# Values turned to token-major on VectorE in 32x32 blocks instead of on TensorE

## The chip, the cores and the metric

One core of one Trainium2 chip runs the whole kernel. A core has a matrix engine (TensorE, PE in the profile), two elementwise engines (VectorE, DVE; ScalarE, ACT), a third for small jobs (GpSimd, POOL), and queues that start transfers (SyncE, SP). Each engine takes its instructions in the order in which they were written for it. The metric is the device time of one execution in microseconds (us). Before the change the median of three runs is 1335.77 us (1335.68 to 1336.22).

## The reference, cut to what matters

A two-layer block over 272 tokens (16 learned ones and 256 of the input; the reference pads them to 384 and masks the padding) with 1024 features. In each layer a normalised input is multiplied by a wide matrix, and the slices of the product feed three branches:

```python
proj = (hn @ w_in).astype(F32)
rq, rk, rv, rg, hq, hf, hi, hg, dq, dk, dv, mg = jnp.split(proj, offs, axis=-1)
o_ret = retention(rq, rk, rv, rg, ...)       # 4 heads, values of 256
o_hg  = hgrn2(hq, hf, hi, hg, lb, ...)       # 8 heads, gated recurrence
o_da  = diff_attention(dq, dk, dv, ...)      # 8 heads, two softmax maps each
y = sum(sigmoid(mg) * (branches @ w_branch)) @ w_out
```

A convolutional feed-forward part with inner width 2816 follows, and a last norm after the second layer. What matters here are the values `rv`, `hi` and `dv`, 1024 features each per layer. Every branch ends in a sum over tokens, "scores times values" (`einsum('bhqk,bkhe->bqhe', s, vc)` and the like), so the values must lie with tokens on the partitions.

## The kernel before, in words

All activations lie feature-major: 128 features on the partitions, 272 tokens along the row. `products` (L780) computes one pair of feature tiles: for each of 8 input tiles and each of the two outputs (16 weight tiles) it issues three matmuls of 272 columns (L801 to L803), since each weight tile is split into a rounded part `whi` and a rest `wlo`. Weights come in chunks of 8 tiles: a transfer into `wraw`, an ACT copy to `whi`, a DVE subtraction to `wlo` (L524 to L526); `wraw` has three buffers, `whi` and `wlo` four each (L516 to L518). Two chunks serve one call of `products`.

A value pair comes out of `products` into PSUM. `values` (L1271) copies it to `vsrc` (128 partitions, two tiles of 272 tokens) and calls `to_tokens` (L837), which turns the first 256 tokens: four 128x128 blocks. The last 16 tokens go another way: POOL copies them to `tails`, and `tail_tokens` (L846) turns those of all heads together on PE. There are four value pairs each of `rv`, `hi` and `dv` per layer, so 24 calls of `to_tokens` in the kernel. They write `rvt` (read by `ret_head`, L911) and `vt` tiles (read by `hg_outputs`, L1106, and `da_head`, L1159).

The work of the branches runs in between the products. `hg_heads` (L949) handles four heads in seven levels (`LEVELS`, L34): at each level PE makes small block products into `lev` (L992), DVE copies parts of them out into `near` or `at`, and then DVE multiplies parts of `hq` and `hf` in place by running decays `tot` (L1074 to L1084); the next level's block products read what was multiplied.

The order of instructions isn't written out but planned on the host before the kernel is issued. Each operation becomes an `_Op` with an engine, an estimated cost and a key (a due time in us on a clock that counts the products only). `order` (L354) plays the five engines forward: an engine takes the ready operation that can start first, and of several the one with the lowest key. A result needed on another engine counts as there 0.4 us later (`CROSS`, L263). The costs are fixed formulas (L478 to L495): a DVE operation 0.068 us plus 1.042 ns per element of a row, a main product group of three matmuls 3 x (columns/2400 + 0.003) us, and

```python
            elif method == "transpose":
                cost = 0.11
```

whatever the engine. The weight chunks have keys 6 us before they are due (`LEAD`, L519), the operations of `to_tokens` about 1 us after the end of their product (L807, L1275); those of the branches are spread over the stretch from `+name` to `!name` in `ORDER` (L58, `behind` and `settle`, L1242 and L1256), and one branch part of a chain starts only after the one before it has been planned. Whatever the plan believed, on the chip each engine keeps the planned order and waits where a result is late. Where the plan keeps track of overlaps (`_span`, L286), it treats a view as the whole stretch of the row between its first and last element.

PSUM has two buffers for small products (`bank`, L589), used in turn by the transposed values, the levels, scores and means.

Of the kernel before, what the change touches and what calls it, by code (L numbers as in the profile page):

```python
# [14 lines left out]
AF = mybir.ActivationFunctionType  # L15
# [4 lines left out]
P = 128  # L20
# [526 lines left out]
def _trace(ctx, tc, plan, a, depth, probe):  # L547
    nc = tc.nc
    act = _Engine(plan, nc.scalar, "act", 0.094, 0.833e-3)
    dve = _Engine(plan, nc.vector, "dve", 0.068, 1.042e-3)  # L550
    pe = _Engine(plan, nc.tensor, "pe", 0.0, 4 / 2400)
# [15 lines left out]
    def new(pool_, shape, dt, tag, bufs, name):  # L567
        serial[0] += 1
        return plan.tile(pool_, shape, dt, tag, bufs, f"{name}_{serial[0]}")
# [16 lines left out]
    def temp2(tag, bufs=2):  # L586
        return temp(2 * T, tag, bufs).rearrange("p (a t) -> p a t", a=2)

    def bank(name):  # L589
        return new(bp, [P, 512], F32, "bank", 2, name)  # L590
# [34 lines left out]
    ident = const[:, C_IDENT : C_IDENT + P]  # L625
# [210 lines left out]

    def to_tokens(src, vt, e):  # L837

        pt = bank("vt").rearrange("p (f c e) -> p f c e", f=2, c=2)
        for f in range(2):  # L840
            for c in range(2):
                pe.transpose(pt[:, f, c, :], src[:, f, c * P : (c + 1) * P], ident)
        for f in range(2):
            act.activation(vt[:, :, e + f * P : e + (f + 1) * P], pt[:, f], AF.Copy)

    def tail_tokens(tails):  # L846

# [28 lines left out]
    for li in range(depth):  # L876
# [389 lines left out]
        def block(name):  # L1266
            if name not in st:
                st[name] = slot4(name)
            return st[name]

        def values(ps, vt, e):  # L1271

            src = temp2("vsrc")
            evacuate(src, ps)
            plan.key += 2.0  # L1275
            to_tokens(src, vt, e)
            return src
# [57 lines left out]
        for name, j in ORDER:  # L1335
# [18 lines left out]
            elif name[0] == "*":  # L1354
# [4 lines left out]
                else:  # L1359
                    t = st["rg" if n == "b0" else "hg"]  # L1360
# [6 lines left out]
            if name in BASE:  # L1367
# [18 lines left out]
                elif name in ("dq", "dk"):  # L1386
                    t = block(f"{name}{j // 2}")
# [3 lines left out]
                elif name == "rv":  # L1391
# [3 lines left out]
                    src = values(ps, st["rvt"][j // 2], (j % 2) * 2 * P)  # L1395
# [4 lines left out]
                elif name in ("hi", "dv"):  # L1400
# [7 lines left out]
                    src = values(ps, st[f"{n}t{b}"], (j % 2) * 2 * P)  # L1408
# [6 lines left out]
                else:  # L1415
                    t = block(f"{name}{j // 2}")
# [31 lines left out]
            elif name == "fi":  # L1448
# [9 lines left out]
                c = temp2("two_b")  # L1458
# [8 lines left out]
                c = c[:, :, first:]  # L1467
# [43 lines left out]
```

## Time and profile before

| | us |
|---|---|
| median of three runs | 1335.77 |
| the profiled execution | 1335.99 |
| its span, first to last instruction | 1334.2 |
| PE busy | 1324.1 |
| DVE busy | 962.0 |
| ACT busy | 813.7 |
| POOL busy | 82.8 |

The span is the profiled execution without some 1.8 us around it. The engines work beside each other, so the busy times don't add up; the engine whose work and waits fill the span sets the time. In the rows, L496 is the line of the helper through which nearly all DVE, ACT, POOL and small PE instructions are issued, so that they must be told apart by the tiles that they write and read (`out<-in`), not by the line. PE matmuls overlap each other in the record: a row gives how long one was under way, while the chain of work gives by how much each moved the end.

### The profile page before, as it was taken

The numbers are of one execution on the slowest core, as the hardware profiler recorded it, in microseconds if no ns is written. First come the engines' busy times: TensorE is split into PE (matmuls) and PEld (weight loads), VectorE is DVE, ScalarE is ACT, GpSimd is POOL, SyncE is SP. The second block draws the span as 40 slices with busy tenths as digits, with TensorE's granted clock in tenths as the row PEclk, the third lists the DMA queues.
The fourth block names the chain that finished last, engine by engine and source line by source line (L and its number), as shares of the span: only waits on it lengthen the run. The fifth ranks groups of instructions, "written<-read, shape, count | busy, mean of one in ns | idle before, by whom it ended". The sixth has DMA issues, their size and how long they took to land.

```text
span 1334.2 us, 28652 instructions
## 1 busy us (share of the span) xinstructions
PE 1324.1 (99%) x11734; PEld 1296.1 (97%) x11734; DVE 962.0 (72%) x1628; ACT 813.7 (61%) x1371; POOL 82.8 (6%) x162
## 2 busy tenths in 40 slices
PE   9999999999999999999999999999999999999998
PEld 9999999999999999999999999999999999999986
DVE  7575777697676789786564757776985867898753
ACT  6747454756576567665446474547566775776643
POOL 5000000000010020000030000000011100200000
PEclk9999999999999999999999999999999999999999
DMA  7644544443544545555555445434445446466653
GB/s 269 192 143 157 161 160 127 137 148 127 175 142 159 174 157 176 180 169 184 176 177 178 157 148 170 161 127 143 143 150 169 143 157 204 143 205 189 194 189 109
DMA packets 60754, 219.05 MB, mean 164 GB/s; under 512 B 6864, under 2 KB 6992, under 8 KB 60624
## 3 DMA queue, kind: packets, MB, share of 16 engines
q1 hardware_dynamic: 60336, 216.71, 49.9%
q8 instruction: 92, 1.51, 0.5%
q10 hardware_dynamic: 288, 0.52, 0.1%
q14 instruction: 38, 0.31, 0.1%
HBM read 216.16 MB, written 1.05 MB: 163 GB/s over the span
## 4 chain that ended last, share of the span: by engine, by line
PE 94%; DVE 4%; issue 1%; ACT 0%; DMA 0%; SPq 0%; DVEq 0%
PE main L801 27%; PE main L802 27%; PE main L803 27%; PE lev L992 2%; PE fo L1311 2%; PE fo L1313 2%; PE fo L1312 2%; DVE two_b L496 1%; DVE wlo L496 1%; PE ds L1176 1%; PE ms L496 1%; PE do L496 1%; PE ro L496 1%; PE ho L496 1%; PE vt L496 1%
## 5 line engine op out<-in xcount | busy, mean ns | idle before, releaser
L801 PE MATMUL main<-xh,whi 128*128 128x272 f32 (+1 forms) x2368 | 694.0, 293 | 0.0
L802 PE MATMUL main<-xl,whi 128*128 128x272 f32 (+1 forms) x2368 | 677.5, 286 | 2.4 <-DVE xl L496 2.4
L803 PE MATMUL main<-xh,wlo 128*128 128x272 f32 (+1 forms) x2368 | 677.4, 286 | 0.3 <-DVE wlo L496 0.2
L496 DVE TENSOR_TENSOR wlo<-wraw,whi 128x1024 fp32r<-128x1024 f32 (+1 forms) x406 | 496.5, 1228 | 203.7 <-ACT whi L496 202.6
L496 ACT ACTIVATE whi<-wraw 128x1024 fp32r<-128x1024 f32 (+1 forms) x406 | 426.4, 1052 | 235.3 <-PE main L802 164.6
L802 PEld LDWEIGHTS main<-xl,whi 128*128 128x128 f32 x2368 | 446.2, 188 | 3.7 <-DVE xl L496 3.0
L801 PEld LDWEIGHTS main<-xh,whi 128*128 128x128 f32 x2368 | 445.6, 188 | 1.6
L803 PEld LDWEIGHTS main<-xh,wlo 128*128 128x128 f32 x2368 | 445.1, 188 | 1.4 <-DVE wlo L496 1.3
L496 DVE SCALAR_TENSOR_TENSOR two_b<-main,small,two_b 128x256 f32<-128x256 f32 (+2 forms) x144 | 65.4, 487 | 30.0 <-ACT two_b L496 28.3
L496 ACT ACTIVATE two_b<-main,small 128x272 f32<-128x272 f32 (+1 forms) x72 | 37.3, 565 | 28.6 <-PE main L803 28.6
L496 POOL TENSOR_TENSOR y<-h,rstd 128x272 f32<-128x272 f32 x32 | 34.8, 1120 | 317.6 <-ACT rstd L496 317.6
L802 PE MATMUL main<-glo,whi 128*128 128x272 f32 x176 | 50.8, 289 | 0.0
L803 PE MATMUL main<-ghi,wlo 128*128 128x272 f32 x176 | 50.7, 288 | 0.0
L801 PE MATMUL main<-ghi,whi 128*128 128x272 f32 x176 | 50.6, 288 | 0.0
L496 ACT ACTIVATE vsrc<-main 128x544 f32<-128x544 f32 x24 | 15.0, 626 | 40.0 <-PE main L803 39.9
L801 PE MATMUL main<-b0hi,whi 128*128 128x272 f32 (+1 forms) x128 | 38.1, 298 | 0.0
L801 PE MATMUL main<-b1hi,whi 128*128 128x272 f32 (+1 forms) x128 | 38.0, 297 | 0.0
L496 POOL COPY tails<-vsrc 128x32 f32<-128x32 f32 x32 | 8.4, 277 | 464.2 <-ACT vsrc L496 464.2
L802 PE MATMUL main<-ylo,whi 128*128 128x272 f32 (+1 forms) x128 | 36.6, 286 | 0.0
L802 PE MATMUL main<-b2lo,whi 128*128 128x272 f32 (+1 forms) x128 | 36.6, 286 | 0.0
L802 PE MATMUL main<-b1lo,whi 128*128 128x272 f32 (+1 forms) x128 | 36.6, 286 | 0.0
L803 PE MATMUL main<-b0hi,wlo 128*128 128x272 f32 (+1 forms) x128 | 36.6, 286 | 0.0
(248 smaller groups left out, 1968.4 us busy)
## 6 DMA issues: line engine op xcount, KB each, us to landing
wraw<-in_w SPq DMA_DIRECT2D x402, 512.0 KB, 3.4
h<-in_h SPq DMA_DIRECT2D x4, 272.0 KB, 5.3
dec<-in_dec SPq DMA_DIRECT2D x2, 544.0 KB, 5.4
wraw<-in_w SPq DMA_DIRECT2D x4, 256.0 KB, 4.4
const<-in_const SPq DMA_DIRECT2D x1, 937.0 KB, 8.4
gain<-in_gl SPq DMA_DIRECT2D x1, 512.0 KB, 5.1
out<-y ACTq DMA_DIRECT2D x2, 256.0 KB, 2.8
out<-y SPq DMA_DIRECT2D x2, 256.0 KB, 2.8
```

What stands on the lines that cost most here:

```text
L496: self.plan.add(self.name, lambda: f(*args, **kw), cost, outs, ins, args[2] if method == "activation" else None)
L801: nc.tensor.matmul(o, wh, hi, start=first, stop=False)
L802: nc.tensor.matmul(o, wh, lo, start=False, stop=False)
L803: nc.tensor.matmul(o, wl, hi, start=False, stop=last)
L992: nc.tensor.matmul(o, keys, x, start=True, stop=True)
L1176: nc.tensor.matmul(ss[m][:, at : at + nk], q[half, hd, q0 : q0 + P], k[half, hd, :nk], start=True, stop=True)
L1311: nc.tensor.matmul(o, gh, wh, start=False, stop=False)
L1312: nc.tensor.matmul(o, gl, wh, start=False, stop=False)
L1313: nc.tensor.matmul(o, gh, wl, start=False, stop=end)
```

## The change

`to_tokens` no longer uses PE, PSUM and ACT. A 256-token, two-tile block of `src` is taken as 4 x 4 groups of 32 partitions by 32 token columns. For each pair (i, j) one DVE instruction reads the 32 partitions of group i, token columns j of each of the 2 x 2 blocks, turns the four 32x32 blocks, and writes them to the partitions of group j, feature columns i. That makes 16 instructions of 32 partitions by 128 elements for each call, reading `vsrc` and writing `vt` or `rvt` directly.

```diff
     def to_tokens(src, vt, e):
 
-        pt = bank("vt").rearrange("p (f c e) -> p f c e", f=2, c=2)
-        for f in range(2):
-            for c in range(2):
-                pe.transpose(pt[:, f, c, :], src[:, f, c * P : (c + 1) * P], ident)
-        for f in range(2):
-            act.activation(vt[:, :, e + f * P : e + (f + 1) * P], pt[:, f], AF.Copy)
+        lanes = [slice(32 * i, 32 * i + 32) for i in range(4)]
+        to = vt[:, :, e : e + 2 * P].rearrange("p c (f e) -> p f c e", f=2)
+        x = src[:, :, : 2 * P].rearrange("p f (c t) -> p f c t", c=2)
+        for i in lanes:
+            for j in lanes:
+                dve.transpose(to[j, :, :, i], x[i, :, :, j])
```

The planner and its costs are as before, so each of the 16 instructions is planned at 0.11 us, and the whole order is planned anew.

## The prediction

> **What bounds the kernel now.** I read the page first: span, busy times, chain.
>
> ```profile
> span 1334.2 us, 28652 instructions
> PE 1324.1 (99%) x11734; PEld 1296.1 (97%) x11734; DVE 962.0 (72%) x1628; ACT 813.7 (61%) x1371; POOL 82.8 (6%) x162
> ...
> PE 94%; DVE 4%; issue 1%; ACT 0%; DMA 0%; SPq 0%; DVEq 0%
> ```
>
> PE is at work for 99% of the span and holds 94% of the chain that ended last. So whatever is taken off PE's queue comes off the time, one for one, as long as PE then has nothing to wait for. Second, the waits of PE:
>
> ```profile
> PE main L802 <- DVE xl L496: 2.4, 3, 1.3
> PE warm L496 <- POOL ones_d L496: 1.0, 1, 1.0
> PE main L803 <- DVE wlo L496: 0.2, 1, 0.2
> ```
>
> PE hardly ever waits for VectorE today (2.4 + 0.2 us), although VectorE is busy for 72% of the span. That is what the change puts at stake: it takes work off the bound engine and gives more work to the one that feeds it. Third, the chain of waits around a call, with the first and the last call in it:
>
> ```profile
> 76.88 0.44 PE vt L496 x4
> ...
> 161.81 0.12 PE main L803
> 161.94 0.44 PE vt L496 x4
> 162.38 0.13 PE main L801
> ...
> 1013.14 0.44 PE vt L496 x4
> ```
>
> The four transposes of a call move the end by 0.44 us and stand between main matmuls of 0.12 to 0.13 us without a gap.
>
> **What the change removes.** The instructions of the turned values:
>
> ```profile
> L496 PE MATMUL vt<-const,vsrc x96: 270/272/273, 76.7 to 1013.3; 128*128 128x128 f32 x96
> ...
> L496 ACT ACTIVATE vt<-vt x32: 368/380/405, 77.4 to 1013.9; 128x256 f32<-128x256 f32 x32
> ...
> L496 ACT ACTIVATE rvt<-vt x16: 363/381/388, 175.7 to 868.2; 128x256 f32<-128x256 f32 x16
> ```
>
> 96 transposes are 24 calls, so PE gets back 24 x 0.44 = 10.6 us, the whole gain. The 48 ACT copies (48 x 0.38 = 18 us) go from an engine at 61%; I cost them at nothing, since PE's list above has no wait for ACT. The `bank` buffer that each call held is free for levels and scores, also worth nothing, since PE's waits name no PSUM buffer. [...]
>
> **What it adds.** 24 x 16 = 384 DVE instructions of 32 partitions by 128 elements. No transpose runs on DVE today; the nearest rows are copies of just that shape, and the longer ones for the price of a column:
>
> ```profile
> L496 DVE COPY at<-lev 32x128 f32<-32x128 f32 x8 | 2.3, 282 | 2.1 <-PE lev L992 2.0
> ...
> 202.32 0.28 DVE L496 COPY at<-lev 32x128 f32<-32x128 f32 x1 [0.20 <-PE lev L992]
> 202.53 0.67 DVE L496 TENSOR_TENSOR hq<-hq,tot 128x512 f32<-128x512 f32 x1
> ...
> L496 DVE TENSOR_TENSOR wlo<-wraw,whi 128x1024 fp32r<-128x1024 f32 x402 | 492.9, 1232 | 202.6 <-ACT whi L496 201.5
> L496 DVE TENSOR_TENSOR hf<-hf,tot 128x544 f32<-128x544 f32 x12 | 8.7, 727 | 3.8 <-PE lev L992 3.7
> ```
>
> The copy is under way for 0.28 us, but the next instruction, which doesn't need it, starts 0.21 us after it. A column costs (1232 - 727)/(1024 - 544) = 1.05 ns. A turned block can't give its first row before its 32nd column is in, so I add 32 columns, 0.03 us, to the 0.21: **0.24 us each**, an estimate from these rows. Lower end 0.21 (the turning costs nothing), upper end 0.28 + 0.03 = 0.31 (each waits for the end of the one before). At 0.24 a call is 3.9 us, all 24 are 93 us, and DVE comes to 962 + 93 = 1055 us, 80% of the span. On average that fits; what matters is where the calls lie, and that the planner reckons with 0.11 x 16 = 1.8 us a call. What it foresees it can place (it moves branch work back and lets PE go on with products); what it doesn't, 16 x 0.13 = 2.1 us a call, makes DVE late against the order that both engines keep.
>
> Busy time by stage, first layer, cut at the starts of the calls:
>
> ```profile
> core 0: us, PE busy (x) PEld busy (x) DVE busy (x) ACT busy (x) POOL busy (x), PEclk, DMA share, GB/s
> 76.60:108.00 31.40, 31.40 (x586) 30.12 (x585) 23.51 (x40) 15.06 (x31) 0.64 (x4) 1.00 0.39 129
> 161.80:175.10 13.30, 13.30 (x110) 13.30 (x109) 7.63 (x12) 7.93 (x16) 0.81 (x3) 1.00 0.48 164
> 175.10:198.90 23.80, 23.80 (x478) 22.88 (x477) 19.92 (x34) 12.36 (x28) 1.61 (x5) 1.00 0.48 161
> 198.90:215.00 16.10, 16.10 (x176) 15.66 (x175) 12.76 (x23) 8.23 (x16) 0.00 (x0) 1.00 0.36 106
> 255.00:271.00 16.00, 16.00 (x132) 16.00 (x131) 11.03 (x21) 12.98 (x26) 0.81 (x3) 1.00 0.47 156
> 342.80:366.00 23.20, 23.20 (x189) 23.20 (x187) 12.26 (x10) 13.12 (x20) 1.41 (x4) 1.00 0.54 184
> ...
> 842.30:866.00 23.70, 23.70 (x478) 22.79 (x477) 19.90 (x34) 12.27 (x28) 1.67 (x6) 1.00 0.49 162
> ```
>
> The calls per stretch are 2, 2, 3, 1, 2, 2, and VectorE's idle time 7.9, 5.7, 3.9, 3.3, 5.0 and 10.9 us. The last row is the third again in the second layer, the same within 0.1 us, so I work one layer out and double it. How late VectorE may be is read where PE needs it soonest, at the levels of `hg_heads`: the multiplication of `hf` ends, then the next level starts on PE.
>
> ```profile
> 190.74 0.72 DVE L496 TENSOR_TENSOR hf<-hf,tot 128x544 f32<-128x544 f32 x1
> 194.31 0.72 DVE L496 TENSOR_TENSOR hf<-hf,tot 128x544 f32<-128x544 f32 x1
> ...
> 192.75 0.67 PE lev L992 x52
> 196.24 0.67 PE lev L992 x52
> ```
>
> 192.75 - 191.46 = 1.3 us and 196.24 - 195.03 = 1.2 us: a cushion of **1.2 us**. Beyond it, the level stands at the head of PE's queue and all main matmuls wait behind it. The `wlo` chunks have a larger cushion (four buffers of eight tiles, each tile three matmuls of 0.125 us, so 3 us a chunk), and I cost them at nothing; if that cover went, main matmuls would wait at L803.
>
> Per layer, then:
>
> - 161.8 to 198.9, two `hi` and three `rv` calls, the last three among the levels of the second four heads. Idle 5.7 + 3.9 = 9.6 us; foreseen 5 x 1.8 = 8.8 us, so 0.8 us is left. Unforeseen 5 x 2.1 us; but the levels rank first (their keys are overdue, they start only when the previous part is planned), so about one call's worth of transposes slips behind the last level, where it makes no level late. 4 x 2.1 - 0.8 - 1.2 = **6.4 us**. Lower end 0 (most slips behind the levels), upper end 5 x 2.1 - 2.0 = 8.5.
> - 76.6 to 108, two `hi` calls among the levels of the first four heads: 2 x 3.9 = 7.8 in 7.9 us of idle time, so VectorE catches up, but a call can be late at once by 2.1 - 1.2 = 0.9 us. I take that once, **0.9** (0 to 1.8).
> - 198.9 to 215, one call, 3.9 in 3.3: counted as the call that slips, **0**. 255 to 271, two `dv` calls: foreseen 3.5 in 5.0, the unforeseen 4.2 against 1.5 left and 1.2 of cushion, 1.5 at most; no levels lie here, so **0.5**. 342.8 to 366: 7.8 in 10.9, **0**.
>
> 7.8 us a layer, 15.6 us in all, against 10.6 gained: +5.0 us on the profiled execution's 1335.99 (its span and 1.8 us around it), so 1341.0; that execution lies 0.2 us over the median of 1335.77, and I say **1341 us**. The same sum with 0.21 us each (1.6 unforeseen: 4.4 + 0.4 + 0, 9.6 in both layers) gives 1335, with 0.28 (2.7: 8.8 + 1.5 + 1.5, 23.6) 1349.
>
> **The rivals.** *Faster:* the extra VectorE time lies in idle time after all. For it: VectorE idles for 202.6 us ahead of `wlo`, for want of `whi` (row above), and the planner fills such gaps with transposes while the levels go first; against it: in 175.1 to 198.9 only 3.9 us are idle for three calls. PE then gets its 10.6 us and waits no more than now: 1335.99 - 10.6 = 1325. It decides when PE's new waits stay under 5.3 us a layer. *Serial transposes:* each instruction pays its whole latency, 0.31 us, 5.0 us a call, 3.2 unforeseen. 4 x 3.2 - 2.0 = 10.8, with 2.0 and 2.0 in the other two stretches 14.8 a layer, 29.6 - 10.6 = +19: 1355. For it: the 0.28 us of the copy. Against it: the 0.21 us to its successor, and that the 16 write separate places. [...] *No change:* the two sides cancel, as at 0.21 us each, 1335.
>
> **How the numbers follow.** About 0.2% (2.7 us) is what a measurement of this kernel can tell from no change. Forecast, waits of 7 to 12 us a layer (1339 to 1349): 0.38. Faster, all or most hidden (1325 to 1333): 0.34. Cancelling within 0.2%: 0.12. Serial, or late for another reason by more than 12 us a layer (1350 and over): 0.16. So slower 0.54, same 0.12, faster 0.34. The likeliest case's own range is 1338 to 1349; the range over the cases runs from just above the full gain, 1326, to the serial sum, 1355. A freshly planned order may add a few us of either sign that no row here prices.
>
> **What would show it.** PE's instructions fewer by 96 and no `vt<-const,vsrc` among them; 384 DVE transposes, 0.21 to 0.24 us from start to start; DVE busy near 1055. Among the waits of PE `lev` for `hf`, `hq` or `near` should be new, in the stretches that answer to 161.8 to 215 and 829 to 882, some 6 us each, and `main L803` for `wlo` still small. I am wrong if PE's idle time stays near 10 us (then faster), if the transposes stand 0.3 us or more apart (then the serial sum), or if PE's new waits are for `wlo`.

## The result and the profile after

The changed kernel takes 1383.64 us (median of four runs, 1382.57 to 1385.62) where the kernel before takes 1335.72 (with a fourth run beside the three above): 1.0359 times as long, 95% interval 1.0346 to 1.0371. That is 47.9 us slower, where 5 us slower was forecast, and far above the range's upper end of 1355. The profiled execution is 1384.09 us. The first lines of its page, with the shares of the chain that ended last:

```profile
span 1382.3 us, 28773 instructions
PE 1329.8 (96%) x11638; PEld 1296.0 (94%) x11638; DVE 1072.3 (78%) x2012; ACT 802.7 (58%) x1323; POOL 84.0 (6%) x162
...
PE 77%; DVE 18%; issue 2%; ACT 1%; DMA 0%; SPq 0%; DVEq 0%; ACTq 0%
```

PE issues the 96 instructions fewer, and yet it is busy 5.7 us longer than before and idle for 52.5 us (1382.3 - 1329.8) instead of 10.1. VectorE now holds 18% of the chain instead of 4%. Whom PE waits for (total us, times, longest):

```profile
PE main L803 <- DVE wlo L496: 13.9, 13, 1.8
PE lev L992 <- DVE hq L496: 11.3, 4, 3.5
PE lev L992 <- DVE hf L496: 7.2, 6, 1.3
...
PE main L802 <- DVE xl L496: 2.4, 3, 1.3
PE ms L496 <- DVE hsl L496: 2.3, 1, 2.3
...
```

Before, the list held the `xl` row and 0.2 us for `wlo`. The level waits are those that the prediction looked for; the largest single row is the one for `wlo`, which it costed at nothing. The added instructions, by their tile (duration min/median/max in ns), and VectorE in order of time at the first call and ahead of the levels of the second four heads (start, length in us):

```profile
L496 DVE STREAM_TRANSPOSE vt<-vsrc x256: 292/303/309, 76.7 to 1067.1; 32x128 f32<-32x128 f32 x128
```

```profile
76.65 5.04 DVE L496 STREAM_TRANSPOSE vt<-vsrc 32x128 f32<-32x128 f32 x16
81.73 1.22 DVE L496 TENSOR_TENSOR wlo<-wraw,whi 128x1024 fp32r<-128x1024 f32 x1
82.87 0.72 DVE L496 TENSOR_TENSOR hq<-hq,he 128x544 f32<-128x544 f32 x1
...
172.86 5.05 DVE L496 STREAM_TRANSPOSE vt<-vsrc 32x128 f32<-32x128 f32 x16
...
183.55 2.18 DVE L496 STREAM_TRANSPOSE rvt<-vsrc 32x128 f32<-32x128 f32 x7
185.76 0.73 DVE L496 TENSOR_TENSOR hq<-hq,he 128x544 f32<-128x544 f32 x1
```

Sixteen transposes take 5.04 us: (5.04 - 0.30)/15 = 0.316 us from start to start, and 0.30 us long each, so one begins only when the one before has ended. Often a whole call stands as one block, ahead of a `wlo` chunk and of the multiplication of `hq` that a level waits for. What PE does meanwhile, by stretches (us, busy us and instructions of each engine, then the granted TensorE clock):

```profile
core 0: us, PE busy (x) PEld busy (x) DVE busy (x) ACT busy (x) POOL busy (x), PEclk, DMA share, GB/s
80.00:84.10 4.10, 1.91 (x55) 1.72 (x56) 4.00 (x9) 0.48 (x2) 0.00 (x0) 1.00 0.03 8
84.10:87.50 3.40, 3.40 (x56) 3.34 (x43) 3.33 (x7) 1.66 (x4) 0.76 (x4) 0.50 0.78 265
183.00:186.50 3.50, 0.04 (x1) 0.00 (x0) 3.39 (x12) 0.94 (x2) 0.00 (x0) 1.00 0.23 95
186.50:189.90 3.40, 3.36 (x74) 3.30 (x75) 3.22 (x10) 1.71 (x3) 0.32 (x1) 0.50 0.02 5
285.50:288.90 3.40, 3.40 (x18) 3.40 (x17) 3.33 (x5) 0.71 (x2) 0.00 (x0) 0.50 0.27 59
```

From 183.0 to 186.5 PE stands still while VectorE works without a pause, and in the 3.4 us that follow PE runs at half its clock. The same comes after other waits: six stretches, one of them of 6.8 us, 23.8 us in all, at a granted clock of 0.50. So in these places PE first waited and then worked slowly, which no term of the prediction held.

### The profile page after: what moved, and what is told of

It reads as the page before. It is cut to its first block, busy times and chain, and to the rows that moved or that the text cites. A ratio compares the mean times of both kernels' runs of the same rounds, so it can differ in the third digit from the quotient of the medians.

```text
span 1382.3 us, 28773 instructions
## 1 busy us (share of the span) xinstructions
PE 1329.8 (96%) x11638; PEld 1296.0 (94%) x11638; DVE 1072.3 (78%) x2012; ACT 802.7 (58%) x1323; POOL 84.0 (6%) x162
## 4 chain that ended last, share of the span: by engine, by line
PE 77%; DVE 18%; issue 2%; ACT 1%; DMA 0%; SPq 0%; DVEq 0%; ACTq 0%
PE main L801 22%; PE main L803 22%; PE main L802 22%; DVE wlo L496 5%; DVE vt L496 4%; DVE rvt L496 2%; PE fo L1311 1%; PE fo L1313 1%; PE fo L1312 1%; DVE two_b L496 1%; DVE hq L496 1%; PE ds L1176 1%; DVE hf L496 1%; PE do L496 1%; PE ho L496 1%
## 5 line engine op out<-in xcount | busy, mean ns | idle before, releaser
L803 PE MATMUL main<-xh,wlo 128*128 128x272 f32 (+1 forms) x2368 | 681.2, 288 | 13.9 <-DVE wlo L496 13.9
L496 DVE STREAM_TRANSPOSE vt<-vsrc 32x128 f32<-32x128 f32 x256 | 77.5, 303 | 6.9 <-ACT vsrc L496 3.5
L496 POOL COPY tails<-vsrc 128x32 f32<-128x32 f32 x32 | 11.8, 383 | 497.7 <-ACT vsrc L496 491.8
L992 PEld LDWEIGHTS lev<-hq,hf 128*32 128x32 f32 (+1 forms) x1248 | 18.5, 118 | 23.3 <-DVE hq L496 9.7
L496 DVE STREAM_TRANSPOSE rvt<-vsrc 32x128 f32<-32x128 f32 x128 | 38.7, 302 | 1.7
L992 PE MATMUL lev<-hq,hf 128*32 128x16 f32 (+2 forms) x1248 | 20.9, 198 | 19.1 <-DVE hq L496 11.3
```

Source lines behind the costliest of these rows:

```text
L496: self.plan.add(self.name, lambda: f(*args, **kw), cost, outs, ins, args[2] if method == "activation" else None)
L803: nc.tensor.matmul(o, wl, hi, start=False, stop=last)
L992: nc.tensor.matmul(o, keys, x, start=True, stop=True)
```

## The experiments

Two theories came first. **A, the order:** the planner prices a transpose at 0.11 us, so it places VectorE's work wrongly; with the true price it would place it where it hurts no one. **B, the room:** VectorE has no place for 5 us a call in the stretches where the calls lie, whatever the order. Beside them stood the question which of the prediction's terms failed, the price of a transpose or the waits that a given price makes.

**The true price for the planner.** Only the order can change:

```diff
-                cost = 0.11
+                cost = 0.315 if self.name == "dve" else 0.11
```

> The changed kernel, with the planner told 0.315 us for a DVE transpose (their spacing in the changed kernel's trace) in place of 0.11. Theory A, the order is to blame (VectorE is late against an order made for 1.8 us a call where it takes 5.0): with true costs the order has room, PE's waits for hf, hq and wlo go, time 1330 to 1348. Theory B, capacity (VectorE is busy for 19.4 of 20 us at 180 to 200, so no order helps): 1365 to 1385.

1372.85 us, 1.0276 (1.0261 to 1.0292) of the kernel before. Of the 48 us, 11 come back. Two of PE's waits, and VectorE in order of time between two calls of the second stretch:

```profile
PE main L803 <- DVE wlo L496: 16.1, 15, 5.3
...
PE lev L992 <- DVE hq L496: 3.2, 1, 3.2
```

```profile
204.52 5.05 DVE L496 STREAM_TRANSPOSE rvt<-vsrc 32x128 f32<-32x128 f32 x16
209.59 2.42 DVE L496 TENSOR_TENSOR wlo<-wraw,whi 128x1024 fp32r<-128x1024 f32 x2
...
212.02 5.05 DVE L496 STREAM_TRANSPOSE rvt<-vsrc 32x128 f32<-32x128 f32 x16
```

The levels wait less and the weight chunks more: two whole calls now stand between the `wlo` chunks. A planner that knows the price moves the wait, and gets rid of little of it. A is worth 11 us in this order.

**The same order, other VectorE work.** Three kernels keep every line of the plan, with its price of 0.11, and put something else in the place of the 16 transposes. The first makes one transpose of 128 partitions by 512 elements of the first and nothing of the other 15; the second makes 16 copies of the same shape; the third makes the one whole transpose and five of the small ones.

```diff
-        for i in lanes:
-            for j in lanes:
-                dve.transpose(to[j, :, :, i], x[i, :, :, j])
+        turn = [lambda: nc.vector.transpose(to, x)] + [lambda: None] * 15
+        for n, (i, j) in enumerate((i, j) for i in lanes for j in lanes):
+            plan.add("dve", turn[n], 0.11, [to[j, :, :, i]], [x[i, :, :, j]])
```

```diff
-                dve.transpose(to[j, :, :, i], x[i, :, :, j])
+                out, src_ = to[j, :, :, i], x[i, :, :, j]
+                plan.add("dve", lambda out=out, src_=src_: nc.vector.tensor_copy(out, src_), 0.11, [out], [src_])
```

```diff
-        for i in lanes:
-            for j in lanes:
-                dve.transpose(to[j, :, :, i], x[i, :, :, j])
+        turn = lambda out, src_: (lambda: nc.vector.transpose(out, src_))
+        for n, (i, j) in enumerate((i, j) for i in lanes for j in lanes):
+            out, src_ = to[j, :, :, i], x[i, :, :, j]
+            run = turn(to, x) if n == 0 else turn(out, src_) if n % 3 == 0 else lambda: None
+            plan.add("dve", run, 0.11, [out], [src_])
```

> The changed kernel's order kept to the instruction on PE, ACT, POOL and SP; the 16 transposes of a call replaced by one of 128 partitions by 512 elements, issued at the place of the first. It leaves out the exchange between the lane groups, so the values are not fully turned. A and B alike (VectorE's time is the cause): 24 calls of about 0.75 us, PE's new waits gone, 1325 to 1329. Theory C, the newly planned order is poor in itself, whatever the transposes take: above 1345. Its one duration beside that of the 16 gives the price of a column and the fixed price: at 1.05 ns a column 0.18 fixed and 0.72 us in all; if the turning itself is slow, over 1 us.

> The changed kernel's order kept; each transpose replaced by a DVE copy of the same 32x128 piece between the same lane groups, at the same planned cost. It leaves out the turning inside the blocks. If the turning makes the instruction slow: copies 0.21 us from start to start as in the kernel before, 3.4 us a call, and the time falls by about half of the loss, to 1345 to 1360. If the small SBUF-to-SBUF shape makes it slow: 0.31 us and 1380 to 1385.

> The changed kernel's order kept on every engine; of the 16 transposes of a call the first is one of 128 by 512 (0.63 us), five more are issued as they stand and ten are left out, so that the values are not fully turned: 0.63 + 5 x 0.315 = 2.2 us a call, 0.4 us more than the 1.76 that the planner foresees. In this same order 0.63 us a call gave 1325.5, 3.7 gave 1355.0 and 5.04 gave 1383.6. If the loss is what goes beyond the foreseen 1.76 us: 24 x 0.4 = 10 us at most, less the cushion, so 1325 to 1330. If every us on VectorE counts, foreseen or not (a straight line through the three points from 0.63 on): 1340.

The whole transpose: 1325.46 us, 0.9922 (0.9907 to 0.9937). The copies: 1355.04, 1.0140 (1.0123 to 1.0157). One whole and five small: 1330.67, 0.9960 (0.9946 to 0.9975). The page of the whole transpose and its waits:

```profile
span 1323.9 us, 28414 instructions
PE 1313.6 (99%) x11638; PEld 1285.4 (97%) x11638; DVE 975.5 (74%) x1652; ACT 802.5 (61%) x1323; POOL 81.5 (6%) x162
```

```profile
PE main L802 <- DVE xl L496: 2.4, 3, 1.3
...
PE main L803 <- DVE wlo L496: 0.2, 1, 0.2
```

These are PE's waits of the kernel before. So the new plan by itself does no harm, and without VectorE's extra time the kernel gains 10.4 us: the 10.6 of the prediction. PE does here the same 11638 instructions as in the changed kernel, which makes this the kernel to subtract: of the 58.4 us between the two spans, 42.2 are PE's idle time (52.5 against 10.3) and 16.2 are PE taking longer over the same work (1329.8 against 1313.6).

What one call costs VectorE, from its order of time in the whole and in the copied kernel:

```profile
77.11 0.70 DVE L842 STREAM_TRANSPOSE vt<-vsrc 128x512 f32<-128x512 f32 x1
77.74 1.18 DVE L496 TENSOR_TENSOR wlo<-wraw,whi 128x1024 fp32r<-128x1024 f32 x1
```

```profile
77.11 3.70 DVE L845 COPY vt<-vsrc 32x128 f32<-32x128 f32 x16
```

0.63 us to the next start for the whole one, 3.70 for the copies ((3.70 - 0.22)/15 = 0.232 us each), 5.04 for the transposes, and for one whole and five small 0.63 + 5 x 0.316 = 2.2. With one order this gives the time against the dose:

| VectorE per call, us | time, us | above the whole transpose | per us of VectorE time added since the row above (24 calls) |
|---|---|---|---|
| 0.63 | 1325.46 | | |
| 2.2 | 1330.67 | 5.2 | 5.2 / 37.7 = 0.14 |
| 3.70 | 1355.04 | 29.6 | 24.4 / 36.0 = 0.68 |
| 5.04 | 1383.64 | 58.2 | 28.6 / 32.2 = 0.89 |

The 2.2 of the second row is added up; at the first call its trace has 2.34 us to the next start (76.78 to 79.12), and with that the rates are 0.13 and 0.75. Up to about 2 us a call, what the plan reckons with (1.8), the time is nearly free; beyond that most of every microsecond ends up in the span. The stretch that holds 8 of a layer's 12 calls, first in the whole, then in the copied, then in the changed kernel:

```profile
161.00:300.00 139.00, 139.00 (x1423) 135.95 (x1422) 112.18 (x218) 80.57 (x146) 5.15 (x17) 1.00 0.44 146
```

```profile
161.00:300.00 139.00, 131.87 (x1345) 127.24 (x1344) 122.93 (x307) 74.15 (x123) 4.60 (x15) 1.00 0.41 136
```

```profile
161.00:300.00 139.00, 123.34 (x1251) 118.49 (x1251) 122.29 (x278) 66.87 (x109) 4.32 (x14) 0.98 0.39 123
```

VectorE's own work there is 112.2 - 8 x 0.63 = 107.1 us of 139. With 8 x 5.04 us it is 147.5: more than the stretch has. That is B, and it holds at any order that leaves this work in the stretch. But it is no more than 8.5 us a layer of the loss, 17 of 58, and the copies, 107.1 + 29.6 = 136.8, would fit and still cost PE 7.1 us in this window. In both overloaded kernels VectorE is busy for 122 to 123 us only: it waits in turn (in the changed kernel 4.7 us for `whi` from ACT and 5.4 us for PE are its longest waits here), so the room that is left isn't all used.

**Later, and out of the way.** The true price, the transposes due 15 us later, and a second source buffer for the third and fourth pairs, so that a late turn doesn't hold up the product behind it:

```diff
-            src = temp2("vsrc")
+            src = temp2(tag)      # "two_a" for the later pairs of hi and rv
...
+            plan.key += 15.0
             to_tokens(src, vt, e)
+            plan.key -= 15.0
```

> As e1_priced (true cost of a transpose in the planner), and the transposes' keys 15 us later, so that they rank behind wlo and fill idle time; the sources of the third and fourth pair of hi and rv lie in the two buffers of another tile (two_a), so that a waiting transpose holds up no evacuation. Theory P, the place in the order (in e1_priced two calls of 5 us each stood ahead of the wlo that PE waited for): 1335 to 1350. Theory B, no room: from 161 to 300 us of the kernel before VectorE is busy for 105 us, and the eight calls there take 40 more, 145 against 135 us of PE's work: at least 10 us a layer, 1350 to 1370.

1369.84 us, 1.0254 (1.0239 to 1.0269): 14 of 48 us back at best, 3 of them by the later dates and the second buffer together. The stretch of the first two calls is clean now, and the loss lies behind it (columns as above):

```profile
76.00:112.00 36.00, 36.00 (x622) 34.71 (x621) 33.65 (x76) 18.26 (x34) 0.92 (x5) 1.00 0.36 119
163.00:214.00 51.00, 44.91 (x582) 43.44 (x580) 48.32 (x109) 19.68 (x32) 3.38 (x7) 1.00 0.39 126
214.00:255.00 41.00, 36.41 (x346) 34.66 (x347) 35.45 (x85) 17.05 (x31) 0.00 (x0) 0.88 0.37 119
255.00:330.00 75.00, 69.19 (x531) 67.77 (x531) 65.31 (x151) 45.20 (x85) 3.38 (x13) 0.95 0.40 129
```

PE is idle for 0, 6.1, 4.6 and 5.8 us in the four. So the two orders made with the true price bring back 0.23 and 0.29 of the loss; no other order was tried, so what the best order could bring is not shown.

**One kind of value alone.** The calls of one branch are turned on VectorE, those of the other two on PE as before:

```diff
-    def to_tokens(src, vt, e):
+    def to_tokens(src, vt, e, kind):
+        if not (kind[:2] == "dv"):      # or "hi", or "rv"
...
+            return
```

> Only the eight dv calls on VectorE, the hi and rv calls on PE and ACT as before, costs as in the changed kernel. From the places where the changed kernel fell behind: about 6 and 1 us a layer, so 1335.7 + 14 = 1350 (1345 to 1354). By the prediction's term for the dv calls (0.5 us a layer against 1.8 gained): 1333.

> Only the eight hi calls on VectorE, planned at 0.11 us as in the changed kernel. From where the changed kernel fell behind: about 4.5 us a layer among the first levels, and 0.9 gained a layer at the second two calls, where no level lies: 1335.8 + 7 = 1343. By the prediction's terms (0.9 us a layer and part of 6.4, against 3.5 gained): 1334 to 1340.

> Only the eight rv calls on VectorE, planned at 0.11 us. If the parts add up: 48 for all, less 10.7 for dv (measured) and 7 for hi, leaves 30: 1366. If the lateness of the hi calls just ahead is carried into the levels (the parts don't add up): 1350 to 1360. By the prediction's term (at most 6.4 us a layer against 1.8 gained): 1345.

| turned on VectorE | time, us | ratio (interval) | against before | waits per layer, with the 1.8 us that PE gains | the prediction's term |
|---|---|---|---|---|---|
| `dv` | 1346.5 | 1.0079 (1.0064 to 1.0094) | +10.6 | 7.1 | 0.5 |
| `hi` | 1350.7 | 1.0112 (1.0096 to 1.0127) | +14.4 | 9.0 | 0.9 and a part of 6.4 |
| `rv` | 1357.95 | 1.0161 (1.0144 to 1.0178) | +21.7 | 12.6 | the rest of 6.4 |

The three losses add up to 46.7 us, the whole kernel's 47.9: each branch's calls make their own loss, and none needs the others. (`hi` alone missed what was expected of it, 1343, and with it the 1366 for `rv` "if the parts add up": they do add up, with 14.4 for `hi` in place of 7.) What PE waits for most in each, `dv`, `hi`, `rv`:

```profile
PE main L803 <- DVE wlo L496: 3.6, 4, 1.8
PE ms L496 <- DVE hsl L496: 3.5, 3, 2.3
```

```profile
PE lev L1000 <- DVE hq L496: 8.2, 4, 2.2
```

```profile
PE main L803 <- DVE wlo L496: 8.7, 11, 1.7
```

With `dv` there is no level near the calls, but a norm of the branch outputs (`ms`), whose squares VectorE splits into `hsl`: a call in front of that makes PE as late as one in front of a level. With `hi` it is the levels nearly alone, with `rv` the weight chunks most of all.

**The price of a transpose by its form.** One kernel for durations alone. `hi` calls are made of four instructions of 32 partitions by 512 elements, `rv` calls of four of 128 by 128, `dv` calls of one of 128 by 512 and sixteen short ones that stay in their own lanes:

```diff
+        forms = {"h": [(to[i], x[i]) for i in lanes],
+                 "r": [(to[:, :, :, i], x[:, :, :, i]) for i in lanes],
+                 "d": [(vt[i, 0, e + 32 * n : e + 32 * n + P], src[i, 0, 32 * n : 32 * n + P]) for i in lanes for n in range(4)]}[kind[0]]
...
```

> A look at durations alone; the values are left unturned in part, so its time says nothing. hi calls: 4 instructions of 32 partitions by 512; rv calls: 4 of 128 partitions by 128 in the changed kernel's pattern of 32-element pieces; dv calls: one of 128 by 512, then 16 of 32 partitions by 128 in one piece on their own lanes. If few lanes or the crossing of lane groups make the small ones slow, 128 by 128 stands under 0.25 us apart; if the short pieces do, the 128 in one piece; if each transpose pays a fixed 0.18 us when another follows, all of 128 elements stand 0.31 and those of 512 0.71 apart.

1345.33 us in one execution, of which nothing is read. VectorE in order of time, one call of each kind:

```profile
76.99 2.85 DVE L856 STREAM_TRANSPOSE vt<-vsrc 32x512 f32<-32x512 f32 x4
...
191.45 0.88 DVE L856 STREAM_TRANSPOSE rvt<-vsrc 128x128 f32<-128x128 f32 x4
...
253.70 4.62 DVE L856 STREAM_TRANSPOSE vt<-vsrc 32x128 f32<-32x128 f32 x14
```

Start to start: (2.85 - 0.70)/3 = 0.717 us for 32x512, (0.88 - 0.28)/3 = 0.20 for 128x128, (4.62 - 0.30)/13 = 0.33 for 32x128 in its own lanes. With all 128 lanes a transpose (0.28 us long) overlaps the next by some 0.08 us; the 32-lane rows show no overlap. That the few lanes are the reason does not follow: the four pieces of a group in the last row overlap by 96 columns and so depend on each other, and the other 32-lane instructions each begin at another group of 32 lanes than the one before. Copies of 32 lanes don't overlap either: they are 0.22 us long and 0.232 apart, only shorter than a transpose. Two places in the traces tell lanes from groups. In the `dv` kernel the first transpose of one call, which reads and writes the first group, stands alone between instructions on all 128 lanes, which begin at that group too:

```profile
262.90 0.18 DVE L496 TENSOR_TENSOR ho<-ho,am 128x16 f32<-128x16 f32 x1
262.98 0.29 DVE L496 STREAM_TRANSPOSE vt<-vsrc 32x128 f32<-32x128 f32 x1
263.20 0.14 DVE L496 TENSOR_TENSOR ho<-ho,am 128x16 f32<-128x16 f32 x1
263.38 3.78 DVE L496 STREAM_TRANSPOSE vt<-vsrc 32x128 f32<-32x128 f32 x12
```

It begins 0.10 us before its neighbour ends, and the next one begins 0.07 us before it ends; the second transpose, in another group, waits until the 0.14 us are over. And in the kernel before, the copy of the first group from which the prediction took its 0.21 us has a twin 1.5 us later in the third group (the code's `at[64 * n : 64 * n + 32]`, with n = 1):

```profile
203.83 0.29 DVE L496 COPY at<-lev 32x128 f32<-32x128 f32 x1
204.15 0.22 DVE L496 TENSOR_TENSOR extra<-hq,tot 128x64 f32<-128x64 f32 x1
```

Here 0.32 us pass from start to start. So in these rows the overlap goes with the group at which an instruction begins: where that changes from one to the next, none of these overlaps, transpose or copy. The changed kernel agrees: the first transpose of a call begins some 0.08 us before the instruction ahead of it ends, where it doesn't wait for `vsrc`, and the other 15 overlap nothing.

**The exchange on other engines.** If one whole transpose costs 0.63 us, the exchange between lane groups can be made elsewhere: 16 copies into a second buffer, then one VectorE transpose, priced at 0.63. On GpSimd; half on GpSimd and half on ScalarE straight from PSUM; and six on each with four on VectorE:

```diff
-        for i in lanes:
-            for j in lanes:
-                dve.transpose(to[j, :, :, i], x[i, :, :, j])
+        z = temp2("two_a")[:, :, : 2 * P].rearrange("p f (c t) -> p f c t", c=2)
+        for j in lanes:
+            for i in lanes:
+                pool.tensor_copy(z[j, :, :, i], x[i, :, :, j])
+        dve.transpose(to, z)
```

```diff
...
+        for n, (i, j) in enumerate(pieces):
+            out, src_ = z[j, :, :, i], x[i, :, :, j]
+            if n < 4:                                  # the third of the three alone
+                dve.tensor_copy(out, src_)
+            elif n % 2:
+                plan.add("pool", lambda out=out, src_=src_: nc.gpsimd.tensor_copy(out, src_), 0.48, [out], [src_])
+            else:
+                act.activation(out, y[i, :, :, j], AF.Copy)    # y: the product in PSUM
+        dve.transpose(to, z)
```

> One DVE transpose of 128 by 512 a call, planned at its 0.63 us, and ahead of it the exchange between the lane groups by 16 copies of 32 by 128 on GpSimd into a buffer of its own (two_a). The values are fully turned. If the loss is VectorE's time alone and GpSimd (6% busy) has the room: 24 x 16 x 0.35 = 134 us on GpSimd, hidden, and 1325 to 1328, faster than both. If GpSimd's copies hold up VectorE or come too late for the heads: wlo takes longer than 1.23 us, or PE waits for ro, ho and do, 1335 to 1360.

> As e10_exchange, with the 16 pieces of the exchange shared: eight by GpSimd (planned at the 0.48 us that e10 showed), eight by ScalarE straight from PSUM. VectorE keeps one transpose of 128 by 512 a call, 0.63 us. If e10 lost for GpSimd's lateness alone (7 to 9 us a call where products follow each 6 to 8 us): GpSimd now needs 3.8 us a call, ScalarE 8 x 0.2 = 1.6 more and two copies fewer, and the time is 1325 to 1329. If the exchange holds PSUM or the later values hold the heads up: 1335 to 1350.

> As e11_split, with four of the pieces as VectorE copies of 32 by 128 (0.23 us each, 0.9 us a call, which the planner is told), six on ScalarE, six on GpSimd. If VectorE has room for what the planner foresees (e9_half: 2.2 us a call, 5 us lost): 1.55 us a call, 1326 to 1331. If GpSimd's share is what counts: faster than e11_split.

1353.05 us, 1.0130 (1.0114 to 1.0147), on GpSimd; 1390.18, 1.0401 (1.0384 to 1.0419), on two engines; 1383.07, 1.0356 (1.0341 to 1.0372), on three. The copies on GpSimd (busy us and mean ns, then idle time) and PE's waits in that kernel:

```profile
L496 POOL COPY two_a<-vsrc 32x128 f32<-32x128 f32 x384 | 182.9, 476 | 336.2 <-ACT vsrc L496 319.9
```

```profile
PE lev L994 <- DVE hf L496: 10.2, 6, 2.8
PE vm L496 <- POOL tails L496: 6.5, 8, 1.6
```

A call takes GpSimd 16 x 0.476 = 7.6 us, a pair of products takes PE 16 x 3 x 0.125 = 6.0 us; VectorE's one transpose comes late and with it what VectorE does next: PE waits for `hf` again, and now for `tails` behind the copies as well. On ScalarE the copies (192 of them, 0.266 us each) hold the product's PSUM bank, which the next product needs; the first wait of PE in the second of these kernels:

```profile
PE main L801 <- ACT two_a L496: 17.6, 8, 4.4
```

The second lies 40 us above the highest time expected for it, with a mean granted clock of 0.981 (0.991 in the changed kernel). None of the three beats the kernel before. The 1325.5 us of the whole transpose is what such a version would take in that order with the exchange at no cost.

## Why the prediction was wrong

The sign, chance 0.54, was right, and so was the mechanism: PE waits for a VectorE that is late, at the places named and at others that were costed at little or nothing. The size was not: a loss of 15.6 us in waits was forecast, 58.2 came (1383.64 - 1325.46), 42.2 of it idle time of PE.

- **The gain, 24 x 0.44 = 10.6 us:** right, 10.4 with VectorE's extra time taken away. The 0.272 us for which one transpose is under way, 26 us over the 96, were no price here: four back to back moved the end by 0.44 us. The copies off ScalarE and the free `bank` were worth nothing, as costed.
- **"0.24 us each":** wrong, 0.316 us, at the upper end that the text gave (0.31). The step that failed is the choice of the nearest row, a copy that overlaps its successor because both begin at the first lane group; its twin in the third group, 0.32 us to the next start, stood in the same trace. Of the 16 instructions of a call each begins at another group than the one before. That copies in this place come to 0.232 us, close to the 0.24, is luck: they don't overlap, but are 0.22 us long and not 0.28. The 0.03 us added for the turning was an estimate; a transpose is 0.303 us long where the copy in its place is 0.22. The serial rival had the price of the transposes, 0.31 us against 0.316. The length of the row alone doesn't make that price: 128 lanes by the same 128 elements stand 0.20 us apart in the kernel with the other forms.
- **The waits at a given price:** wrong, by half even where the price was right. The copies take 3.70 us a call, a little under the 3.9 of the prediction, and cost 29.6 us where the sum said 15.6. Against the whole transpose PE's idle time grows by 21.4 us there (1353.1 - 1321.4, less 10.3), and PE is busy 7.8 us longer over the same instructions (1321.4 against 1313.6), for which no term stood. At 5.04 us the prediction's own serial sum was 29.6 and the kernel shows 58.2. How the missing 42.6 us divide depends on which is put right first: by the last step of the dose the price brings 28.6 and the working of the waits 14.0; by the prediction's own sums the price brings 14.0 (29.6 - 15.6) and the waits 28.6. Both failed, and neither is the smaller part for certain.
- **"No levels lie here, so 0.5":** wrong; 7.1 us a layer with `dv` alone (PE is idle for 3.8 us from 255 to 300 and for 1.4 us from 342 to 380, for which the sum had 0). The search was for levels only. PE also waits for VectorE at `ms` and at the main matmuls.
- **"The `wlo` chunks have a larger cushion, and I cost them at nothing":** wrong; 13.9 us of listed waits, the largest row. The cushion of 3 us a chunk was worked out against a lateness of 2.1 us; one call is 3.3 us later than planned, and several follow each other. The text said that new waits for `wlo` would prove it wrong, and they do.
- **"2 x 3.9 = 7.8 in 7.9 us of idle time, so VectorE catches up":** wrong. `hi` alone, at its true 5.04 us, loses 9.0 us a layer, and even the copies, at 3.70 us, leave PE idle for 2.45 of the 34 us from 76 to 110, where 0.9 was forecast. A call stands as one block ahead of the one multiplication that PE needs, so the level waits at once; idle time later in the stretch doesn't give that back, and of the 7.9 us of idle time VectorE had spent 5.4 waiting for PE's levels.
- **The clock:** no term had it. Half-clock stretches of 23.8 us, if PE had worked through all of them at full clock, cost at most 12 us of the 16.2 by which PE's work took longer. No run isolates it; the copies, with 29.6 us of loss, have a mean granted clock of 0.998, and the true price has 30.6 us at 0.50 (0.988 on average, 0.991 in the changed kernel) and is faster than the changed kernel, so it is not what decides. The remaining 4 us of longer work are not shown by any run. An estimate: a main matmul is under way for 0.29 us and moves the end by 0.12, so each stop leaves some 0.17 us of standing in the busy time, and 37 waits in its full list, against 6 for the whole transpose, make that 5 us.
- **"The planner's price":** the prediction made the unforeseen part the cause of all waits. The dose says that the foreseen part is nearly free (0.14 per us), but letting the planner foresee the rest brings only 11 of 48 us back, 14 with later dates. The count of room explains some 17 us of what these two orders still lose against the whole transpose (47.4 and 44.4); the rest stays open, since no run has these orders without VectorE's extra time.

The range ended at the serial sum, 1355, and the copies reached just that at the lower price: its top was built with the same wait formula as the forecast, so it could not cover an error in the formula.

## What to carry to other kernels

Price an instruction by a row of its own operation with neighbours like its own (here: does it begin at the same group of lanes as they do?); where there is none, the bound must carry the whole latency. Room on an engine that feeds the bound one is counted stage by stage, with every place where the bound engine reads from it, and not to the full: here the 8 calls of a stretch with 139 - 107.1 = 31.9 us of room were nearly free at 8 x 2.2 us, and each microsecond of a call beyond cost 0.7 to 0.9. Other work of known length in the same planned order tells a wrong price from wrong waits in two runs.

## What the runs showed of the hardware

- The VectorE instructions of 32 lanes looked at here that begin at another lane group than the one before do not overlap it: transposes of 128 elements stand 0.316 us apart (0.303 long), of 512 elements 0.717 (0.70 long), copies of 128 elements 0.232 (0.22 long). A 32-lane transpose in the first group between instructions on all lanes overlaps both, by 0.10 and 0.07 us. Transposes of 128 lanes stand 0.20 us apart and, of 512 elements ahead of a `wlo` subtraction, 0.63 us.
- After waits of PE (for `hq` some 2.2 and 3.5 us in the first two places, for `hsl` 2.3 in the third) its granted clock is 0.50 for 3.4 us (rows above), and a main matmul moves the end by 0.23 us instead of 0.12, as the chain of the changed kernel shows:

```profile
285.38 0.12 PE main L802
...
285.87 0.23 PE main L802
```

  The 4.1 us ahead of the first stretch still hold 1.91 us of PE work; in the last 3.4 us ahead of each of the six PE is busy for 0 to 1.3 us. From 200 to 232, where PE waits six times for 0.6 to 1.7 us, the clock stays at 1.00. What sets the half clock off is not shown.
- A GpSimd copy of 32x128 takes 0.476 us on average, 0.288 in the median and 0.28 at best, while VectorE's `wlo` subtraction of 128x1024 stays at 1235 ns on average (1232 before).
